# Other starting addresses for the FFN weight tiles and for one SwiGLU remainder

## The chip, the cores and the metric

The kernel runs on one core of a Trainium2 chip. The metric is the device time of one execution in microseconds (us). Before the change it is 1229.76 us, the median of two runs (1229.75 and 1229.76).

## The reference

One layer of a hybrid decoder over 256 tokens of width 2048, in float32:

```python
h = rms_norm(x, attn_norm_w)
p = h @ w_in                                   # 2048 x 6920
mixed = concat(rwkv7(p), gated_deltanet(p), differential_attention(p))
x = x + mixed @ w_out                          # 2048 x 2048
h = rms_norm(x, ffn_norm_w)
gate, up = split(h @ w_ffn_in, 2)              # 2048 x 11264
x = x + (silu(gate) * up) @ w_ffn_out          # 5632 x 2048
```

The change touches the last two products alone, the FFN: 11264 columns going in, 5632 rows coming out.

## The kernel before, in words

**Products in three terms.** Every large product is made of rounded operands (type float32r) and their remainders: a value v becomes hi = round(v) and lo = v - hi, and x*w is taken as xh*wh + xh*wl + xl*wh. In each such matmul the activations are the stationary operand (128 x 128, loaded into the array ahead of the matmul) and the weights are the moving operand (128 x 512, streamed through it). The result goes to a bank of PSUM.

**Weight units.** All weights come as a list of 410 units in the order of their use. A unit is 2 x 128 rows by 512 columns (512 KB; some at the start are smaller). `fetch_upto` issues a unit's DMA from SyncE's queue into a tile `raw`; `stage_upto` lets ScalarE round it into `hi` (L245) and VectorE subtract to `lo` (L246); `products` (L320 to L330) multiplies. A unit of the FFN makes 12 matmuls, all at L328: two halves of the tokens (t), two blocks of 128 rows (k), three terms in the order xh with hi, xh with lo, xl with hi. `take` stages three units ahead of the one that is multiplied (LA = 3), and `hi` and `lo` have four buffers each. In the FFN (units from `plan["far"]` on, which is all but its first four) `raw` comes from the pool `ffn` with FAR + 1 = 9 buffers, fetched five units ahead of staging; elsewhere `raw` has four buffers.

**Order of the work.** Start (`rk` and the LoRA columns, 264 wide), then the other columns of `w_in`; beside them RWKV, the delta net and attention run as generators that advance one step behind each unit; then the output projection (oA, oB) with its stationary operands `mixh_a`/`mixl_a` and `mixh_d`/`mixl_d`; then the FFN in two passes (24 and 20 blocks of 128 hidden columns). A pass makes chunks of 512 gate columns and 512 up columns with `hTh`/`hTl` stationary; SwiGLU's result is transposed by `hid_cols` into `hidh` and, as the remainder, `hidl`; then four output chunks of 512 columns run with `hidh`/`hidl` stationary. Nothing in the FFN is ordered by hand beyond this sequence.

**Where tiles lie.** The pools `raw`, `hi`, `lo` (four tiles of 1024 elements, 4096 bytes in each partition) and `hT` (two tiles of 16 x 256 elements) lie one behind the other, and the pool `ffn` opens directly behind `hT` with `hidh`, `hidl` (24 x 256 elements each). All these sizes are multiples of 512 bytes, and so are the steps between blocks of 128 rows inside them. So in the FFN, and in all products with `hTh`/`hTl` ahead of it whose units are 512 wide, the moving and the stationary operand start a whole multiple of 512 bytes apart. Three cases differ. `mixh_a` and `mixl_a` lie behind tiles that end on an odd 128 bytes (`gns` is 2 x 16 elements): they start 128 bytes past such a multiple. `mixh_d` and `mixl_d` start 160 bytes past one. In the 264-wide units of the start the second block of rows starts 1056 bytes into the tile, 32 bytes past a multiple.

```python
hi = p_hi.tile([P, 1024], F32R, tag="hi", name=nm("hi"))     # stage_upto
lo = p_lo.tile([P, 1024], F32R, tag="lo", name=nm("lo"))
r, h, l = raws.pop(u), hi[:, :nk * n], lo[:, :nk * n]
S.copy(h, r)                                                 # L245
V.tensor_tensor(l, r, h.bitcast(F32), op=ALU.subtract)       # L246
```

Of the kernel before, what the change touches and what calls it, by code (L numbers as in the profile page):

```python
# [9 lines left out]
F32R = mybir.dt.float32r  # L10
# [5 lines left out]
P = 128  # L16
T = 256
# [17 lines left out]
AY = 2  # L35
WARM = 5
FIRST = 8
FAR = 8
START = ((0, 1), (1, 1)) + tuple((k, 2) for k in range(2, 16, 2))

SET_NLE = "natural_log_exp_and_others"
# [52 lines left out]


class Acts:
    """Activation calls grouped by the table set that they need."""

    def __init__(self, tc):
        self.tc, self.nc = tc, tc.nc  # L100
# [27 lines left out]
def trunk(tc, A, out, dbg=None):  # L128
# [24 lines left out]
    def nm(s):  # L153
        uid[0] += 1
        return f"{s}_{uid[0]}"
# [13 lines left out]
        tog[0] ^= 1  # L169
        return rwbank() if tog[0] else gdbank()  # L170

    # ------------------------------------------------------------------ constants
    cst = pc.tile([P, CONST.shape[1]], F32, name="cst")
    vec = pc.tile([P, NV], F32, name="vec")

# [22 lines left out]
    rs1, lnr1, rsq64, ss2, rs2 = rst[:, 0:2], rst[:, 2:4], rst[:, 4:6], rst[:, 6:8], rst[:, 8:10]  # L198
    ssq = pc.tile([P, 8], F32, name="ssq")

    # ------------------------------------------------------------------ weight stream
    cm_raw, p_raw = pool("raw", 4)
    cm_hi, p_hi = pool("hi", 4)
    cm_lo, p_lo = pool("lo", 4)
    LA = 3

    units = []
# [6 lines left out]
    raws, staged = {}, {}  # L214
    state = {"fetched": 0, "next": 0}
# [19 lines left out]
    def stage_upto(i):  # L235
        fetch_upto(min(i + FIRST - LA, 2 * len(START) - 1))
        fetch_upto(i + FAR - LA if i >= plan["far"] else i)
        while state["next"] <= min(i, len(units) - 1):
            u = state["next"]
            srcs, nk, ns = units[u]  # L240
            n = sum(ns)
            hi = p_hi.tile([P, 1024], F32R, tag="hi", name=nm("hi"))
            lo = p_lo.tile([P, 1024], F32R, tag="lo", name=nm("lo"))
            r, h, l = raws.pop(u), hi[:, :nk * n], lo[:, :nk * n]
            S.copy(h, r)  # L245
            V.tensor_tensor(l, r, h.bitcast(F32), op=ALU.subtract)  # L246
            staged[u] = (h.rearrange("p (k c) -> p k c", c=n), l.rearrange("p (k c) -> p k c", c=n))
            state["next"] += 1
# [10 lines left out]
    HALF = (24, 20)  # L259
    plan = {"rk": [], "lora": []}  # L260
# [20 lines left out]
        plan["ffn"].append((h0, nh, ins_, outs_))  # L281
        h0 += nh

    # ------------------------------------------------------------------ side work, emitted between weight units
    jobs = []

    def spawn(gen, steps=0):
# [21 lines left out]
            advance(g)  # L309

    def after(first, then):
        """Keep the order of two instructions of one engine."""
        first, then = getattr(first, "ins", first), getattr(then, "ins", then)
        act._dep(then, first)

    def products(banks, ul, i, xs, n=512, parts=False):
        """What unit i of a chunk adds to its banks."""
        u, k0, nk = ul[i]
        wh, wl = take(u)
        if parts:  # L320
            seq = [(t, k, p_) for k in range(nk) for p_ in range(3) for t in range(2)]
        else:
            seq = [(t, k, p_) for t in range(2) for k in range(nk) for p_ in (0, 2, 1)]
        seen = [0, 0]
        for t, k, p_ in seq:
            seen[t] += 1
            xh, xl = xs(k0 + k)
            state["mm"] = TE.matmul(banks[t][:, 0:n], lhsT=(xl if p_ == 1 else xh)[:, t * P:(t + 1) * P],  # L328
                                    rhs=(wl if p_ == 2 else wh)[:, k, :], start=(i == 0 and seen[t] == 1),
                                    stop=(i == len(ul) - 1 and seen[t] == 3 * nk))  # L330

    def proj(ul, xs):
        """One chunk of 512 columns in token layout: two banks."""
        banks = [mmbank(), mmbank()]
        for i in range(len(ul)):
            products(banks, ul, i, xs)
            tick()
        return banks

    def rsq(out_, in_, scale=1.0, bias=None, b2=None):  # L340
        """out = (in*scale + bias)^-1/2 [* exp(b2)]"""
        act(out_, in_, AF.Ln, scale=scale, bias=eps_c[:in_.shape[0]] if bias is None else bias)
        if b2 is None:
            act(out_, out_, AF.Exp, scale=-0.5)
        else:
            act(out_, out_, AF.Exp, scale=-0.5, bias=b2)

    # ------------------------------------------------------------------ start: x and its norm
    cm_hT, p_hT = pool("hT")
    hTh = p_hT.tile([P, KT, T], F32R, name="hTh")  # L350
    hTl = p_hT.tile([P, KT, T], F32R, name="hTl")
# [6 lines left out]
    cm_x, p_x = pool("xp", side="right")  # L358
    x_in = A["x"].rearrange("(t p) d -> t p d", p=P)
    xT_in = A["xT"].rearrange("(k p) t -> p k t", p=P)  # L360
    # the array's clock rises while the first loads are on their way
    V.memset(xs1, 0.0)
    b = rwbank()
    for _ in range(WARM):
# [1 line left out]
    nc.scalar.dma_start(vec, A["vecs"])  # L366
    act.window(SET_NLE)
    def load_x():
        """x, transposed, in step with the units of the first chunks; then the constants."""
        xTs = {}  # L370

        def fetch_x(q):
            if q < len(START):
                k0, n = START[q]
                xTs[q] = p_x.tile([P, 2, T], F32, tag="xT", name=nm("xT"), bufs=FIRST // 2 + 1)
                (nc.sync if q else nc.scalar).dma_start(xTs[q][:, 0:n, :], xT_in[:, k0:k0 + n, :])
                fetch_upto(2 * q + 1)

        for q in range(FIRST // 2):
            fetch_x(q)  # L380
        for q, (k0, n) in enumerate(START):
            fetch_x(q + FIRST // 2)
            xT = xTs.pop(q)
            xsq = p_x.tile([P, 2, T], F32, tag="xsq", name=nm("xsq"), bufs=2)
            for j in range(n):
                k = k0 + j
                S.activation(hTh[:, k, :], xT[:, j, :], AF.Copy, scale=vcol("attn_w", k))
                V.scalar_tensor_tensor(hTl[:, k, :], xT[:, j, :], vcol("attn_w", k), hTh[:, k, :].bitcast(F32),
                                       op0=ALU.mult, op1=ALU.subtract)
            act(xsq[:, 0:n, :], xT[:, 0:n, :], AF.Square)  # L390
            for j in range(n):
                V.tensor_tensor(xs1, xs1, xsq[:, j, :], op=ALU.add)
            if q < 2:
                stage_upto(2 * q + 1)
            if q:
                yield
        nc.sync.dma_start(cst, A["const"])
        yield
        nc.sync.dma_start(lora[0:64, :], A["w_lora_b"])
        nc.sync.dma_start(lora[64:128, :], A["a_lora_b"])  # L400
        nc.sync.dma_start(glora, A["g_lora_b"])

    def first_norm():
# [7 lines left out]
        V.tensor_scalar(rsq64, rsq64, 1.0 / 64.0, None, op0=ALU.mult)  # L411
        V.tensor_scalar(lnr1, lnr1, -0.5, None, op0=ALU.mult)
        yield
        # small derived vectors
        V.tensor_scalar(omu, vcol("mu", 0, 14), -1.0, 1.0, op0=ALU.mult, op1=ALU.add)
        V.tensor_scalar(oka, vcol("k_a", 0, 4), -1.0, 1.0, op0=ALU.mult, op1=ALU.add)
        V.tensor_scalar(qw8, vcol("qn"), 0.125, None, op0=ALU.mult)
# [22 lines left out]
        products(banks_lora, plan["lora"], i, hx, 264, parts=True)  # L440
    close(cm_x)

    # ------------------------------------------------------------------ RWKV
    cm_tok, p_tok = pool("tok")
    cm_rq, prq = pool("rwq")
    sgx = prq.tile([P, T], F32, name="sgx")
# [27 lines left out]
    kk = pe.tile([P, 4, T], F32, name="kk")  # L474
# [10 lines left out]
    G.memset(XT[96:128, :, 0:32], 0.0)  # L485

    def tokens(banks, n=512):
        """Normalised rows of a chunk, one tile per 128 tokens."""
        res = []
        for t in range(2):  # L490
            tk = p_tok.tile([P, 512], F32, tag="tok", name=nm("tok"), bufs=TOKB)
            S.activation(tk[:, 0:n], banks[t][:, 0:n], AF.Copy, scale=rs1[:, t:t + 1])
            res.append(tk)
        return res

    def turned(toks, i, bank):
        """Column tiles 2i, 2i+1 of a chunk, columns on the partitions: bank[:, j*256 + t]."""
        for j in range(2):
            for t in range(2):
                TE.transpose(bank[:, j * T + t * P:j * T + (t + 1) * P],  # L500
                             toks[t][:, (2 * i + j) * P:(2 * i + j + 1) * P], ident)
        return bank
# [9 lines left out]

    KKRv = KKR.rearrange("p a c s t -> p (a c) s t")

    # inverse of the unit triangular blocks of 32, all at once, by forward substitution
    def forward_sub(n, fill, drain, Fa, Fx, Ft, per):
        scr = tc.dram_tile([n, 32, 32], F32, name=nm("scr"))
        scr2 = tc.dram_tile([n, 32, 32], F32, name=nm("scr2"))
# [142 lines left out]
    def rw_recur():  # L661
        V.transpose(X11[64:96, :, :], XT[64:96, :, 0:32])
        yield
        for i in range(2):
            b = rwbank()
            for j in range(16):
                ch = 16 * i + j
                TE.matmul(b[96:128, j * 32:(j + 1) * 32], lhsT=AHf[64:96, ch, 96:128], rhs=X11[64:96, ch, :],  # L668
                          start=True, stop=True, tile_position=(64, 96))
# [12 lines left out]
            return 2 * hp + par  # L682

        def read(c, which, rows):
            """Chunk c's tokens on the rows given: state times (r or kk), plus the part within the chunk."""
            b = rwbank()
            for hp in range(4):
                if c > 0:
# [62 lines left out]
    ready["rr"] = tokens(proj(plan["rr"], hx))  # L751
    ready["rv"] = tokens(proj(plan["rv"], hx))

    # ------------------------------------------------------------------ gated delta net
    banks_z = proj(plan["gz"], hx)
    while "rw_v" not in ready:
        tick()
# [281 lines left out]
            S.activation(mh, bv, AF.Copy, scale=vcol("gn"))  # L1039
            V.scalar_tensor_tensor(ml, bv, vcol("gn"), mh.bitcast(F32), op0=ALU.mult, op1=ALU.subtract)  # L1040

    # ------------------------------------------------------------------ differential attention
    def diff_evac(j, banks, res):
        qns = []
        for t in range(2):
# [138 lines left out]
            dj = spawn(diff_evac(j, banks, res), 1)  # L1184
        ready["d", g] = ops

    # ------------------------------------------------------------------ output projection
    def mixs(k):
        if k < 8:
            return mixh_a[:, k, :], mixl_a[:, k, :]  # L1190
# [46 lines left out]
    for cm in (cm_d, cm_mixrg, cm_rq, cm_tok):  # L1237
        close(cm)

    # ------------------------------------------------------------------ feed forward  # L1240
    cm_f, pf = pool("ffn")
    act.window(SET_SILU)
    out_v = out.rearrange("(t p) d -> t p d", p=P)
# [10 lines left out]

    for fi, (hh0, nh, ins_, outs_) in enumerate(plan["ffn"]):
        hh_ = pf.tile([P, HALF[0], T], F32R, tag="hidh", name=nm("hidh"))
        hl_ = pf.tile([P, HALF[0], T], F32R, tag="hidl", name=nm("hidl"))
        for c, (ug, uu) in enumerate(ins_):
            bg = proj(ug, hx)
            sgs = []  # L1260
# [67 lines left out]
```

## Time and profile before

| | |
|---|---|
| median of the runs | 1229.76 us |
| the profiled execution: span from the first to the last instruction | 1227.3 us |
| TensorE matmul (PE) busy | 1221.7 us, 6062 instructions |
| TensorE weight load (PEld) busy | 1006.7 us |
| VectorE (DVE) busy | 710.2 us |
| ScalarE (ACT) busy | 589.8 us |
| mean granted TensorE clock | 0.999 |

The profiled execution's span is 1227.3 us; the 2.46 us up to the median lie before its first and behind its last instruction. A matmul's busy time in this profile (some 390 ns) is longer than the time after which the next one starts, because matmuls are pipelined; what a row of matmuls costs is read from the distance of their starts, called the pitch below.

### The profile page before, as it was taken

Reading aid. Unit: us, or ns where it says so; the run is one execution under the profiler, and the core shown is the slowest. Engines: PE = TensorE matmul, PEld = TensorE weight load, DVE = VectorE, ACT = ScalarE, POOL = GpSimd, SP = SyncE. Lnnn points to the kernel's source line nnn. Section 1 sums busy time; section 2 is a strip of 40 time slices with the busy share of each in tenths; the row PEclk is TensorE's granted clock in tenths of the full one; section 3 lists DMA queues with packets and bytes.
Section 4 is the critical chain, followed back from the end, with each engine's and each line's share of the span. In section 5 each row is a group of like instructions: output and inputs, shape, how many; then the busy total and the mean of one; then the engine's idle time right before and its main releaser. Section 6 shows DMA issues by size and latency. Waiting matters only on the chain.

```text
span 1227.3 us, 15743 instructions
## 1 busy us (share of the span) xinstructions
PE 1221.7 (100%) x6062; PEld 1006.7 (82%) x6062; DVE 710.2 (58%) x972; ACT 589.8 (48%) x799; POOL 5.8 (0%) x11
## 2 busy tenths in 40 slices
PE   9999999999999999999999999999999999999998
PEld 8887888788888878888888888888888888888887
DVE  8585965699565766554454454544445445545553
ACT  7764454665446556544444444433344444444332
POOL 0100000000000000000000000000000000000000
PEclk9999999999999999999999999999999999999999
DMA  9755564256555545766666666566666666665660
GB/s 323 211 150 157 167 196 118 72 152 187 174 162 188 164 129 172 280 199 189 186 190 190 189 188 191 188 194 196 193 190 189 191 188 188 195 190 185 212 195 34
DMA packets 125082, 222.41 MB, mean 181 GB/s; under 512 B 15664, under 2 KB 19888, under 8 KB 125008
## 3 DMA queue, kind: packets, MB, share of 16 engines
q1 hardware_dynamic: 116848, 217.15, 58.6%
q10 hardware_dynamic: 8160, 4.27, 1.2%
q8 instruction: 47, 0.77, 0.2%
q14 instruction: 27, 0.22, 0.1%
HBM read 218.50 MB, written 2.88 MB: 180 GB/s over the span
## 4 chain that ended last, share of the span: by engine, by line
PE 99%; DMA 1%; ACT 0%; DVE 0%; issue 0%; SPq 0%
PE mm L328 90%; PE rw L500 1%; PE gd L500 1%; PE rw L692 1%; PE rw L622 1%; PE rw L1085 1%; PE rw L689 0%; PE rw L705 0%; DMA xT<-in_xT 0%; PE rw L562 0%; DMA vec<-in_vecs 0%; PE rw L1120 0%; PE gd L1120 0%; PE rw L676 0%; PE rw L668 0%; ACT s L121 0%
## 5 line engine op out<-in xcount | busy, mean ns | idle before, releaser
L246 DVE TENSOR_TENSOR lo<-raw,hi 128x1024 fp32r<-128x1024 f32 (+2 forms) x410 | 493.9, 1208 | 432.8 <-ACT hi L245 429.0
L245 ACT CAST hi<-raw 128x1024 fp32r<-128x1024 f32 (+2 forms) x410 | 425.2, 1039 | 535.3 <-PE mm L328 509.7
L328 PE MATMUL mm<-hi,hTh 128*128 128x512 f32 (+1 forms) x1152 | 448.9, 394 | 0.2
L328 PE MATMUL mm<-hi,hTl 128*128 128x512 f32 (+1 forms) x1152 | 441.4, 388 | 0.0
L328 PE MATMUL mm<-lo,hTh 128*128 128x512 f32 (+1 forms) x1152 | 441.1, 387 | 0.0
L328 PEld LDWEIGHTS mm<-hi,hTh 128*128 128x128 f32 x1152 | 215.6, 188 | 44.6 <-issue 1.1
L328 PEld LDWEIGHTS mm<-hi,hTl 128*128 128x128 f32 x1152 | 215.2, 188 | 45.1 <-issue 0.6
L328 PEld LDWEIGHTS mm<-lo,hTh 128*128 128x128 f32 x1152 | 215.4, 188 | 42.8 <-issue 1.1
L328 PE MATMUL mm<-hi,hidh 128*128 128x512 f32 x352 | 137.3, 390 | 0.0
L328 PE MATMUL mm<-hi,hidl 128*128 128x512 f32 x352 | 137.0, 389 | 0.0
L328 PE MATMUL mm<-lo,hidh 128*128 128x512 f32 x352 | 137.0, 389 | 0.0
L328 PEld LDWEIGHTS mm<-hi,hidl 128*128 128x128 f32 x352 | 66.1, 188 | 13.9
L328 PEld LDWEIGHTS mm<-hi,hidh 128*128 128x128 f32 x352 | 66.1, 188 | 13.6
L328 PEld LDWEIGHTS mm<-lo,hidh 128*128 128x128 f32 x352 | 66.1, 188 | 13.5
L328 PE MATMUL mm<-hi,mixh_a 128*128 128x512 f32 x64 | 26.0, 406 | 0.0
L328 PE MATMUL mm<-hi,mixh_d 128*128 128x512 f32 x64 | 25.9, 408 | 0.0
L328 PE MATMUL mm<-hi,mixl_d 128*128 128x512 f32 x64 | 25.4, 400 | 0.0
L328 PE MATMUL mm<-lo,mixh_d 128*128 128x512 f32 x64 | 25.4, 396 | 0.0
L328 PE MATMUL mm<-hi,mixl_a 128*128 128x512 f32 x64 | 25.3, 395 | 0.0
L328 PE MATMUL mm<-lo,mixh_a 128*128 128x512 f32 x64 | 25.2, 394 | 0.0
L121 ACT ACTIVATE sg<-mm,rst 128x512 f32<-128x512 f32 x22 | 15.2, 691 | 10.7 <-PE mm L328 10.7
L778 DVE SCALAR_TENSOR_TENSOR cacc<-gd,vec,cacc 128x255 f32<-128x255 f32 (+2 forms) x36 | 16.2, 477 | 5.8 <-ACT cacc L776 5.5
(301 smaller groups left out, 729.4 us busy)
## 6 DMA issues: line engine op xcount, KB each, us to landing
raw<-in_w_ffn_in SPq DMA_DIRECT2D x176, 512.0 KB, 3.8
raw<-in_w_in SPq DMA_DIRECT2D x103, 512.0 KB, 3.7
raw<-in_w_ffn_out SPq DMA_DIRECT2D x88, 512.0 KB, 4.5
raw<-in_w_out SPq DMA_DIRECT2D x32, 512.0 KB, 4.0
raw<-in_w_in SPq DMA_DIRECT2D x9, 256.0 KB, 5.7
xr<-in_x SPq DMA_DIRECT2D x8, 256.0 KB, 5.1
out<-xr ACTq DMA_DIRECT2D x8, 256.0 KB, 3.7
xT<-in_xT SPq DMA_DIRECT2D x7, 256.0 KB, 5.6
```

What stands on the lines that cost most here:

```text
L121: r = self.nc.scalar.activation(out, in_, func, **kw)
L245: S.copy(h, r)
L246: V.tensor_tensor(l, r, h.bitcast(F32), op=ALU.subtract)
L328: state["mm"] = TE.matmul(banks[t][:, 0:n], lhsT=(xl if p_ == 1 else xh)[:, t * P:(t + 1) * P], rhs=(wl if p_ == 2 else wh)[:, k, :], star ...
L500: TE.transpose(bank[:, j * T + t * P:j * T + (t + 1) * P], toks[t][:, (2 * i + j) * P:(2 * i + j + 1) * P], ident)
L622: TE.matmul(b[:, hp * P:(hp + 1) * P], lhsT=KB[rows, hp, c, :, :].rearrange("p s t -> p (s t)"), rhs=KKR[rows, hp, c, :, :].rearrange("p s ...
L692: TE.matmul(b[rows, h * 64:(h + 1) * 64], lhsT=AH[:, c, h % 2, h // 2, 64 * which:64 * which + 64], rhs=VU[:, c, h, :], start=(c == 0 and ...
L778: V.scalar_tensor_tensor(acc[:, sft:T], src[:, 0:T - sft], vcol("conv", 4 * ct + 3 - sft), acc[:, sft:T], op0=ALU.mult, op1=ALU.add)
L1085: TE.matmul(bk[m][:, hx_ * W:(hx_ + 1) * W], lhsT=qT[r, h, i * P:(i + 1) * P], rhs=kT_[r, h, 0:W], start=True, stop=True)
```

## The change

In the FFN's units from `plan["far"]` on, `hi` and `lo` come from the pool `ffn` with three buffers each instead of the four of the older pools, and are 64 elements longer (4352 bytes). What a unit writes begins o = 4 * (u // 2 % 16) elements into them, that is 0, 16, 32, ... 240 bytes, one position for two units and all sixteen in 32 units. `raw` of these units has four buffers (FAR = 3) and is fetched when it is staged. `hidl` is 8 elements longer and its content starts 32 bytes into it. All that is allocated in that pool behind `hidl` lies 32 bytes further on as well. The rest of the diff removes comments.

```diff
-FAR = 8
+FAR = 3
...
-            hi = p_hi.tile([P, 1024], F32R, tag="hi", name=nm("hi"))
-            lo = p_lo.tile([P, 1024], F32R, tag="lo", name=nm("lo"))
-            r, h, l = raws.pop(u), hi[:, :nk * n], lo[:, :nk * n]
+            if u >= plan["far"]:
+                hi = pf.tile([P, 1024 + 64], F32R, tag="hif", name=nm("hi"), bufs=3)
+                lo = pf.tile([P, 1024 + 64], F32R, tag="lof", name=nm("lo"), bufs=3)
+                o = 4 * (u // 2 % 16)
+            else:
+                hi = p_hi.tile([P, 1024], F32R, tag="hi", name=nm("hi"))
+                lo = p_lo.tile([P, 1024], F32R, tag="lo", name=nm("lo"))
+                o = 0
+            r, h, l = raws.pop(u), hi[:, o:o + nk * n], lo[:, o:o + nk * n]
...
-        hl_ = pf.tile([P, HALF[0], T], F32R, tag="hidl", name=nm("hidl"))
+        hl_ = pf.tile([P, HALF[0] * T + 8], F32R, tag="hidl", name=nm("hidl"))
+        hl_ = hl_[:, 8:].rearrange("p (k t) -> p k t", t=T)
```

## Rows read from the trace of the kernel before

**Rows 1.** The page's first part: busy time and instructions of each engine.

```profile
PE 1221.7 (100%) x6062; PEld 1006.7 (82%) x6062; DVE 710.2 (58%) x972; ACT 589.8 (48%) x799; POOL 5.8 (0%) x11
```

**Rows 2.** The chain of work that ended last, by engine (page, part 4).

```profile
PE 99%; DMA 1%; ACT 0%; DVE 0%; issue 0%; SPq 0%
```

**Rows 3.** The page's DMA issues: count, size, us from issue to landing.

```profile
raw<-in_w_ffn_in SPq DMA_DIRECT2D x176, 512.0 KB, 3.8
...
raw<-in_w_ffn_out SPq DMA_DIRECT2D x88, 512.0 KB, 4.5
```

**Rows 4.** Stretches of matmuls alone; (x) counts all that reach into a stretch.

```profile
core 0: us, PE busy (x) PEld busy (x) DVE busy (x) ACT busy (x) POOL busy (x), PEclk, DMA share, GB/s
70.50:75.50 5.00, 5.00 (x24) 4.14 (x23) 4.88 (x6) 4.98 (x7) 0.78 (x1) 1.00 0.11 42
801.00:850.00 49.00, 49.00 (x218) 40.58 (x217) 23.42 (x21) 18.99 (x18) 0.00 (x0) 1.00 0.62 192
419.80:426.50 6.70, 6.70 (x30) 5.41 (x29) 4.76 (x9) 4.95 (x18) 0.00 (x0) 1.00 0.23 81
479.80:486.80 7.00, 7.00 (x32) 5.63 (x31) 5.42 (x7) 3.98 (x8) 0.00 (x0) 1.00 0.64 191
```

**Rows 5.** Order of time, first and last matmul of 801 to 850 (start, duration).

```profile
800.65 0.39 PE L328 MATMUL mm<-hi,hidl 128*128 128x512 f32 x1
...
849.84 0.39 PE L328 MATMUL mm<-hi,hidh 128*128 128x512 f32 x1
```

**Rows 6.** Order of time, first and last matmul of 70.5 to 75.5.

```profile
70.25 0.39 PE L328 MATMUL mm<-hi,hTl 128*128 128x512 f32 x1
...
75.46 0.39 PE L328 MATMUL mm<-lo,hTh 128*128 128x512 f32 x1
```

**Rows 7.** Order of time, output projection oA, 419.8 to 426.5.

```profile
419.58 0.39 PE L328 MATMUL mm<-hi,mixl_a 128*128 128x512 f32 x1
419.81 0.40 PE L328 MATMUL mm<-hi,mixh_a 128*128 128x512 f32 x1
420.05 0.39 PE L328 MATMUL mm<-lo,mixh_a 128*128 128x512 f32 x1
...
426.34 0.40 PE L328 MATMUL mm<-lo,mixh_a 128*128 128x512 f32 x1
```

**Rows 8.** Order of time, output projection oB, 479.8 to 486.8.

```profile
479.45 0.39 PE L328 MATMUL mm<-hi,mixh_d 128*128 128x512 f32 x1
...
479.91 0.40 PE L328 MATMUL mm<-hi,mixl_d 128*128 128x512 f32 x1
480.15 0.39 PE L328 MATMUL mm<-hi,mixh_d 128*128 128x512 f32 x1
...
486.68 0.39 PE L328 MATMUL mm<-lo,mixh_d 128*128 128x512 f32 x1
```

**Rows 9.** Order of time at the start, 264 wide; two matmuls of equal operands merged.

```profile
30.62 0.40 PE L328 MATMUL mm<-hi,hTh 128*128 128x264 f32 x2
...
31.34 0.41 PE L328 MATMUL mm<-hi,hTh 128*128 128x264 f32 x2
...
32.07 0.39 PE L328 MATMUL mm<-hi,hTh 128*128 128x512 f32 x1
```

**Rows 10.** Order of time in the FFN behind two transposes.

```profile
543.76 0.38 PE L500 MATMUL rw<-cst,sg 128*128 128x128 f32 x2
543.90 0.48 PE L328 MATMUL mm<-hi,hTh 128*128 128x512 f32 x1
544.21 0.39 PE L328 MATMUL mm<-lo,hTh 128*128 128x512 f32 x1
...
545.83 0.39 PE L328 MATMUL mm<-hi,hTl 128*128 128x512 f32 x1
```

**Rows 11.** The page's costliest groups, staging: busy us, mean ns, idle before, releaser.

```profile
L246 DVE TENSOR_TENSOR lo<-raw,hi 128x1024 fp32r<-128x1024 f32 (+2 forms) x410 | 493.9, 1208 | 432.8 <-ACT hi L245 429.0
L245 ACT CAST hi<-raw 128x1024 fp32r<-128x1024 f32 (+2 forms) x410 | 425.2, 1039 | 535.3 <-PE mm L328 509.7
```

## The prediction

> **What bounds the kernel now.** I read the busy times first: TensorE is busy for 1221.7 of 1227.3 us, no other engine above 58% of the span [rows 1]. Then the chain of waits: 99% of it is TensorE, nothing else reaches 2% [rows 2]. So the time is the number of matmuls times their pitch, and only what changes one of the two counts. The number stays: the FFN is 176 + 88 units [rows 3] of 12 matmuls, 3168 in all.
>
> The pitch I read from the order of time, in stretches without transposes. In the FFN, 218 matmuls reach into 801 to 850 us, the first starts at 800.65, the last at 849.84: 217 steps, 49.19 / 217 = 0.2267 us, at a granted clock of 1.00, the 2.4 GHz level [rows 4, 5]. At 70 us, with the same multiples of 512 bytes between moving and stationary operand, it is 23 steps in 5.21 us, 0.2265, although ScalarE and VectorE are busy there for 4.98 and 4.88 of 5.00 us [rows 4, 6]. The output projection is slower in the same instruction: oA, its stationary operand 128 bytes off such a multiple, takes 29 steps in 6.76 us, 0.2331, with single steps of 0.23 and 0.24 in turn [rows 4, 7]; oB, 160 bytes off, 31 steps in 7.23 us, 0.2332, where two of 0.23 and one of 0.24 repeat [rows 4, 8]. Clock, columns and line are the same; the other engines, busier at 70 us, don't explain it. What differs in the code is where the operands lie against each other. That is an inference from three places, but it is exactly the quantity that this change moves, in 16-byte steps.
>
> **The change, part by part.**
>
> *Longer way through fewer buffers.* Rounding waits for the array to give back a buffer of hi (L245, 509.7 us of idle ended by PE) [rows 11], so with three buffers it starts one unit later, when the unit three before is done. Two units then lie between that and its use: 2 x 12 x 0.2267 = 5.44 us. Rounding and subtracting take 1.04 + 1.21 = 2.25 us [rows 11], so 3.2 us are left, and the work that hides them is two units of matmuls. SiLU, the SwiGLU products and the copies of the transposes stand on the same two engines at each chunk's end; they may take those 3.2 us. If the cover were gone, TensorE would wait at most once a unit for what sticks out. I cost it at 0. Bounds: nothing and, at 22 ends of a gate or up chunk, one rounding of 1.04 us each, 23 us; I take nothing, since both engines sit idle for over 400 us ahead of exactly these instructions [rows 11].
>
> *Four raw buffers.* A raw tile comes free when its remainder is formed, and the next DMA into it is issued then, on SyncE's queue, where only other weight loads stand. It lands 3.8 to 4.5 us later [rows 3]. By the order above it is issued 2.25 us after the end of unit v - 7 and needed for rounding at the end of unit v - 3, that is 4 x 2.72 = 10.9 us: 4.1 us of cover remain. Cost 0. The copies' and subtractions' start addresses change too; neither engine bounds anything.
>
> *The addresses.* The first four FFN units keep the old tiles, so 260 x 12 = 3120 matmuls get moving operands at o = 0 to 240 bytes; buffers of 4352 bytes (17 x 256) and a pool moved by 32 bytes add multiples of 32. So against hTh/hTl, and against hidh, all 16-byte positions within 256 bytes occur, equally often as far as the list of units goes round; hidl stands 32 bytes from where hidh stands. The pitch at most positions isn't in the trace. The nearest rows: 226.7 ns at 0, 233.1 at 128, 233.2 at 160. For 32 bytes there are only matmuls of 264 columns: six from 30.62 to 31.34 at distance 0 and six up to 32.07 at 32 bytes, 0.72 and 0.73 us [rows 9], so about 1 ns more each. None of these is below the value at 0.
>
> I take the mean of the three 512-column values, 231.0 ns, for the sixteen positions: zero is one of them and may have good neighbours, as the 264-wide rows say, and the two far ones agree. That is 4.3 ns x 3120 = 13 us. A second effect points the same way: after a disturbance the pitch needs several matmuls to settle. Behind two transposes the first takes 0.31 us, and the seven steps from 544.21 to 545.83 average 0.231 before 0.227 returns [rows 10]. Each new position (every two units) disturbs it anew; that holds up a good position as much as the mean already does, so I add nothing.
>
> Bounds of a matmul: above, the slow step of oB, 0.24 us by the rounded starts [rows 8], held throughout would be some 11 ns x 3120 = 34 us. Below, 512 columns without any fixed part: from 264 to 512 columns the pitch rises from 0.12 (0.72 / 6) to 0.2267, 0.43 ns a column, or 220 ns for 512, 6.9 ns less each, -21 us.
>
> Sum against the profiled execution: 1227.3 + 13 = 1240.3 us of span; 2.46 us lie around it up to the median of the runs, which makes 1243.
>
> **Rivals.**
>
> *Addresses don't matter.* The slower pitch of the output projection would then come from something else there. For it: attention runs beside oA. Against: oB keeps the pattern, and 70 us is as busy. The time would be that of before, 1228 to 1232; chance 0.16. The Trainium skill speaks for this one: by "SBUF — State Buffer", section "Who interferes with whom", TensorE has two SBUF read ports, one for the moving operand and one for the weight load, independent of each other, and never waits on another engine. By that rule the position could cost nothing and the sum would be 0. The two pitches of rows 5 and 7 are the measurement that it leaves unexplained.
>
> *Distance zero is the bad case and most positions are free.* Both operands then meet in the same part of the memory at 0, and 128 and 160 bytes happen to meet it again; an offset of 16 to 112 bytes keeps them apart. For it: 226.7 ns is above the 220 of the columns alone, so something is being paid at 0. Against: all three other distances seen are slower. It decides if more than about half of the positions lie below 226.7 ns. At 220 to 225 the FFN gains 1.7 to 6.7 ns a matmul, 5 to 21 us: 1209 to 1225; chance 0.16. The same skill, "TensorE: Matmul & The Clock Gate", section "Back-to-back issue gap", gives an estimate further down, about 216 ns for 512 columns, -34 us; no row here goes that low.
>
> *Never settled, and late staging.* Every move of the position throws the pitch up to between oB's mean and its slow step, 235 to 238 ns, and two units are too short to come back: 8 to 11 ns x 3120, 25 to 34 us. Or the chunk ends stick out by 1 us each: 13 + 23 = 36 us. Either way 1254 to 1266; chance 0.12. For it: seven matmuls to settle out of 24. Against: they average 231 [rows 10], not 235.
>
> **How the numbers follow.** The forecast, a pitch between 229 and 234 averaged over the FFN (1236 to 1253), has 0.56; likeliest 1243. The range 1222 to 1255 takes in the forecast, the case without effect, the mild part of the gain and the start of the late one; outside lie about 0.10 below and 0.10 above. A measurement of this kernel tells about 2% (24.6 us) from no change: 0.05 for faster than 1205, since even 220 ns throughout gives 1209; 0.13 for slower than 1254; the rest within.
>
> **What would show it.** After: stretches of FFN matmuls whose pitch changes every second unit (24 matmuls) with the position, and returns after 32 units; a mean near 231 with clock 1.00; 227 where the distance is 0 and 233 near 128 and 160; the stages before the FFN unchanged to 1 us; no idle time of TensorE behind rounding or DMA. I am wrong if the pitch stays at 226.7 at every position, if some positions lie well below it, or if TensorE waits for hi, lo or raw.

## The result and the profile after

The changed kernel takes 1245.51 us (1245.22 to 1245.81, two runs) against 1229.76: 1.0128 times as long, 95% interval 1.0085 to 1.0172. Forecast was 1243 in a range of 1222 to 1255. The profiled execution has a span of 1243.4 us, 16.1 more than before; the sum had 1240.3.

Busy times, the chain of waits by engine and the two staging groups of the changed kernel:

```profile
PE 1236.4 (99%) x6062; PEld 1006.8 (81%) x6062; DVE 710.0 (57%) x972; ACT 588.5 (47%) x799; POOL 5.8 (0%) x11
...
PE 99%; DMA 1%; ACT 0%; DVE 0%; SPq 0%; issue 0%; ACTq 0%
...
L252 DVE TENSOR_TENSOR lo<-raw,hi 128x1024 fp32r<-128x1024 f32 (+2 forms) x410 | 493.8, 1208 | 452.6 <-ACT hi L251 452.0
L251 ACT CAST hi<-raw 128x1024 fp32r<-128x1024 f32 (+2 forms) x410 | 423.8, 1036 | 562.3 <-PE mm L334 537.6
```

Same number of matmuls, 14.7 us more of TensorE, nothing else busier [rows 1, 2, 11]: rounding and subtracting at the shifted starts take 1036 and 1208 ns as before. All time in which TensorE waited, with its releaser (total, times, longest):

```profile
PE rw L371 <- DVE xs L368: 1.2, 1, 1.2
PE mm L334 <- ACT hi L251: 1.1, 1, 1.1
PE mm L334 <- ACT hTh L393: 0.7, 1, 0.7
```

Each occurs once, in the first 40 us; in the FFN TensorE waits for nothing. Now the FFN's first and last matmul in order of time, first of the kernel before, then of the changed one:

```profile
493.61 0.40 PE L328 MATMUL mm<-hi,hTh 128*128 128x512 f32 x1
...
1222.99 0.39 PE L328 MATMUL mm<-hi,hidl 128*128 128x512 f32 x1
```

```profile
493.99 0.40 PE L334 MATMUL mm<-hi,hTh 128*128 128x512 f32 x1
...
505.85 0.40 PE L334 MATMUL mm<-hi,hTh 128*128 128x512 f32 x1
...
511.49 0.39 PE L334 MATMUL mm<-hi,hTh 128*128 128x512 f32 x1
...
517.08 0.40 PE L334 MATMUL mm<-hi,hTh 128*128 128x512 f32 x1
...
522.53 0.40 PE L334 MATMUL mm<-hi,hTh 128*128 128x512 f32 x1
...
528.01 0.39 PE L334 MATMUL mm<-hi,hTh 128*128 128x512 f32 x1
...
533.57 0.40 PE L334 MATMUL mm<-hi,hTh 128*128 128x512 f32 x1
...
607.89 0.40 PE L334 MATMUL mm<-hi,hTh 128*128 128x512 f32 x1
...
613.34 0.40 PE L334 MATMUL mm<-hi,hTh 128*128 128x512 f32 x1
...
1239.13 0.40 PE L334 MATMUL mm<-hi,hidl 128*128 128x512 f32 x1
```

What ran before the FFN differs by 0.38 us. The FFN takes 745.14 us against 729.38: 15.76 us more, all of the change. The FFN's weight tiles step through their positions from 505.85 on. The rows from there to 533.57 are the first matmuls of successive pairs of units, 24 matmuls apart. In the allocated layout the moving operand lies 208 bytes past the stationary one (modulo 256) from 505.85 on, then 224, 240, 0 and 16. The five stretches last 5.64, 5.59, 5.45, 5.48 and 5.56 us: a pitch of 235.0, 232.9, 227.1, 228.3 and 231.7 ns. The pitch steps with the position, and in these input products the old 226.7 [rows 5] is kept, but for the first matmuls that settle, at 240 and 0 alone (176 and 192 always have transposes among their matmuls here, 48 and 64 but once). One round of the list later the distances are the same but for a multiple of 256 bytes, and so is the stretch at 240: 5.45 us from 607.89.

The output products keep it nowhere. Here is their pair with `hidh` at distance 0, where `hidl` lies 32 bytes off:

```profile
795.06 0.40 PE L334 MATMUL mm<-hi,hidh 128*128 128x512 f32 x1
...
800.66 0.39 PE L334 MATMUL mm<-hi,hidh 128*128 128x512 f32 x1
```

It takes 5.60 us, 233.3 ns a matmul.

A stretch of output products, columns as in rows 4:

```profile
820.00:850.00 30.00, 30.00 (x131) 24.34 (x130) 14.35 (x13) 11.54 (x11) 0.00 (x0) 1.00 0.59 186
```

The granted clock is 1.00 as before, and the 30 us hold some 129 matmuls where 226.7 ns would give 132.

### The profile page after: what moved, and what is told of

Its sections match the earlier page's. It is cut to its first block, busy times and chain, and to the rows that moved or that the text cites. A ratio compares the mean times of both kernels' runs of the same rounds, so it can differ in the third digit from the quotient of the medians.

```text
span 1243.4 us, 15743 instructions
## 1 busy us (share of the span) xinstructions
PE 1236.4 (99%) x6062; PEld 1006.8 (81%) x6062; DVE 710.0 (57%) x972; ACT 588.5 (47%) x799; POOL 5.8 (0%) x11
## 4 chain that ended last, share of the span: by engine, by line
PE 99%; DMA 1%; ACT 0%; DVE 0%; SPq 0%; issue 0%; ACTq 0%
PE mm L334 90%; PE rw L506 1%; PE gd L506 1%; PE rw L698 1%; PE rw L628 1%; PE rw L1091 1%; PE rw L695 0%; DMA raw<-in_w_in 0%; PE rw L711 0%; PE rw L568 0%; DMA vec<-in_vecs 0%; PE rw L1126 0%; PE gd L1126 0%; PE rw L682 0%; PE rw L674 0%; ACT s L121 0%
## 5 line engine op out<-in xcount | busy, mean ns | idle before, releaser
L252 DVE TENSOR_TENSOR lo<-raw,hi 128x1024 fp32r<-128x1024 f32 (+2 forms) x410 | 493.8, 1208 | 452.6 <-ACT hi L251 452.0
L251 ACT CAST hi<-raw 128x1024 fp32r<-128x1024 f32 (+2 forms) x410 | 423.8, 1036 | 562.3 <-PE mm L334 537.6
```

## Experiments

All edits are against the changed kernel or the kernel before, as said. Times are compared with the kernel before on the same chip.

**Buffers alone.** The changed kernel without its two shifts (the tiles keep their 64 spare elements):

```diff
-                o = 4 * (u // 2 % 16)
+                o = 0
...
-        hl_ = pf.tile([P, HALF[0] * T + 8], F32R, tag="hidl", name=nm("hidl"))
-        hl_ = hl_[:, 8:].rearrange("p (k t) -> p k t", t=T)
+        hl_ = pf.tile([P, HALF[0], T], F32R, tag="hidl", name=nm("hidl"))
```

> The changed kernel without any shift: three hi and lo buffers and four raw buffers from the pool of the FFN, but every unit begins at the start of a 1024-element tile and the SwiGLU remainder isn't moved, so moving and stationary operand of the FFN lie multiples of 256 bytes apart again. Theory (the distance between the two operands sets the pitch): FFN pitch 226.7 ns at every unit, time 1230 us (1228 to 1232). Rival (the shorter way through fewer buffers costs the time): pitch 226.7 ns with waits of TensorE for hi or raw, 1240 to 1246 us.

Measured 1229.88 us, ratio 0.9997 (0.9988 to 1.0006). Its first and last matmul of the FFN:

```profile
494.81 0.40 PE L334 MATMUL mm<-hi,hTh 128*128 128x512 f32 x1
...
1224.19 0.39 PE L334 MATMUL mm<-hi,hidl 128*128 128x512 f32 x1
```

729.38 us, the same as before to 0.01 us. Three buffers and the short fetch cost nothing; the rival falls. What is left is the place of the operands.

**The remainder alone.** The kernel before, with hidl's 32 bytes as in the change and nothing else.

> The kernel before with the remainder hidl moved by 32 bytes alone. Theory: only the 1056 matmuls of the FFN's output products change. Where the changed kernel had hidh at distance 0 and hidl 32 bytes beside it, its three terms took 231.4, 232.0 and 235.2 ns, 232.9 on the mean, so 6.2 ns x 1056 = 6.5 us: 1236 us (1234 to 1238). Rival (only the moving tiles' own start counts): 1230 us.

Measured 1236.87 us, 1.0048 (1.0036 to 1.0061). The three terms in order of time:

```profile
800.85 0.40 PE L328 MATMUL mm<-hi,hidh 128*128 128x512 f32 x1
801.08 0.40 PE L328 MATMUL mm<-lo,hidh 128*128 128x512 f32 x1
801.32 0.39 PE L328 MATMUL mm<-hi,hidl 128*128 128x512 f32 x1
...
803.65 0.40 PE L328 MATMUL mm<-hi,hidh 128*128 128x512 f32 x1
```

Twelve matmuls from 800.85 to 803.65 take 2.80 us, 233.3 ns each. The moving tiles are untouched; where the stationary operand lies counts too, at the price that was forecast.

**One far position.** The first experiment with `o = 52` (208 bytes) for every unit.

> The layout of the first experiment, but every unit from the fifth of the FFN on begins 208 bytes into its tile: one fixed distance in place of sixteen. Theory: the distance holds a pitch of its own; at 208 bytes the changed kernel's three terms took 234.9, 234.9 and 234.5 ns, so 8.1 ns x 3120 = 25 us, 1255 us (1252 to 1258), the same at the end of a chunk as at its start. Rival (moving from one position to the next disturbs the pitch, a fixed one settles back to 227 ns): 1230 us, at most 1233.

Measured 1252.38 us, 1.0177 (1.0163 to 1.0191), at the lower end of the 1252 to 1258 expected. A stretch of matmuls alone and its first and last:

```profile
810.00:850.00 40.00, 40.00 (x172) 32.11 (x171) 18.47 (x16) 14.92 (x15) 0.00 (x0) 1.00 0.58 184
```

```profile
809.66 0.40 PE L334 MATMUL mm<-lo,hidh 128*128 128x512 f32 x1
...
849.78 0.40 PE L334 MATMUL mm<-lo,hidh 128*128 128x512 f32 x1
```

171 steps in 40.12 us, 234.6 ns, 40 us long without a move: a position holds its own pitch. It isn't the moving from one to the next that costs.

**A map of pairs.** The first experiment with separate starts for hi and lo.

```diff
-                o = 0
+                j = (u - plan["far"]) // 2
+                o, ol = 4 * (j % 16), 4 * ((j // 16 + 0) % 16)
...
-            r, h, l = raws.pop(u), hi[:, o:o + nk * n], lo[:, o:o + nk * n]
+            r, h, l = raws.pop(u), hi[:, o:o + nk * n], lo[:, ol:ol + nk * n]
```

> The layout of the first experiment with separate starts for hi and lo: hi moves by 16 bytes every two units, lo by 16 bytes every 32 units (0 to 112 bytes), so that 128 pairs of distances are seen for two units each. Theory: pitch by the distance of each moving tile from the stationary operand loaded beside it; 226.7 ns where both are 0, some 229 to 236 ns elsewhere, 1243 to 1249 us. It is open whether a pair lies below 226.7 ns: by the theory that 0 is the best distance none does; by the rival that something is still being paid at 0, some reach 220 to 225 ns.

One run: 1245.14 us. The two quickest pairs of units, hi and lo both at 0, and hi at 192 with lo at 16, each with the start of the pair behind it:

```profile
506.49 0.39 PE L335 MATMUL mm<-hi,hTh 128*128 128x512 f32 x1
...
511.93 0.39 PE L335 MATMUL mm<-hi,hTh 128*128 128x512 f32 x1
...
664.64 0.39 PE L335 MATMUL mm<-hi,hTh 128*128 128x512 f32 x1
...
670.09 0.40 PE L335 MATMUL mm<-hi,hTh 128*128 128x512 f32 x1
```

5.44 and 5.45 us for 24. No pair was quicker, so the second rival of the prediction (0 is the bad distance) has no position on its side. Only half of lo's positions were tried, and pairs with transposes among their matmuls can't be compared. The second of the two pairs also tells against the theory: neither of its moving tiles is at distance 0 or 240, and it is as quick as those.

**One operand, the other, both.** The first experiment, with the output products' weight tiles 48 bytes on (`o = 12` for units of w_ffn_out), with hidh and hidl 48 bytes on, and with both. For both:

```diff
-                o = 0
+                o = 12 if units[u][0][0].tensor is w_fo.tensor else 0
...
-        hh_ = pf.tile([P, HALF[0], T], F32R, tag="hidh", name=nm("hidh"))
-        hl_ = pf.tile([P, HALF[0], T], F32R, tag="hidl", name=nm("hidl"))
+        hh_ = pf.tile([P, HALF[0] * T + 64], F32R, tag="hidh", name=nm("hidh"))
+        hh_ = hh_[:, 12:12 + HALF[0] * T].rearrange("p (k t) -> p k t", t=T)
+        hl_ = pf.tile([P, HALF[0] * T + 64], F32R, tag="hidl", name=nm("hidl"))
+        hl_ = hl_[:, 12:12 + HALF[0] * T].rearrange("p (k t) -> p k t", t=T)
```

> The layout of the first experiment with the weight tiles of the FFN's output products alone begun 48 bytes later; hidh and hidl stay. Theory (the distance between moving and stationary operand sets the pitch, with a period of 256 bytes): distance 48; at 48 the input products of the changed kernel took 233.6, 232.3 and 233.2 ns, so 6.4 ns x 1056 = 6.7 us, 1236 to 1237 us. Rival (the start of the moving operand by itself counts): the same here.

> The layout of the first experiment with hidh and hidl begun 48 bytes later; the weight tiles stay at the start of theirs. Theory: distance -48, which is 208 of 256 bytes; the pitch there was 234.8 ns, 8.1 x 1056 = 8.6 us, 1238 to 1239 us. Rival (only the moving operand's own start counts): 1230 us.

> The layout of the first experiment with both operands of the FFN's output products begun 48 bytes later: the distance is 0 again, while neither start is where it was. Theory: pitch 226.7 ns, 1230 us (1229 to 1231). Rival (each operand's own start counts, not the distance): 1236 to 1237 us if it is the moving one's, about 1245 us if both cost what they cost alone.

Measured 1232.92 (1.0027, 1.0017 to 1.0038), 1236.65 (1.0056, 1.0044 to 1.0069) and 1235.09 us (1.0046, 1.0032 to 1.0059). The stretch from 801 to 850, in this order:

```profile
801.00:850.00 49.00, 49.00 (x214) 39.99 (x214) 23.36 (x20) 18.41 (x18) 0.00 (x0) 1.00 0.62 192
```

```profile
801.00:850.00 49.00, 49.00 (x211) 39.87 (x210) 22.23 (x20) 18.90 (x18) 0.00 (x0) 1.00 0.61 184
```

```profile
801.00:850.00 49.00, 49.00 (x211) 39.48 (x210) 22.72 (x20) 18.61 (x18) 0.00 (x0) 1.00 0.62 187
```

214, 211 and 211 matmuls reach in where it was 218 [rows 4]. The second came out near its expectation (6.9 of 8.6 us), the first at half (3.3 of 6.7), and the third, 1235 instead of 1230, refutes the theory in its simple form: the distance is 0 and the pitch isn't 226.7. The rivals fare no better (the moving operand's own start would leave the second at 1230; both costs added make 1240). In the stretch shown of the second run nothing that another engine reads or writes starts elsewhere modulo 256 bytes, so it is TensorE's own operand that costs.

The third run shows one thing more. In its second pass the starts are the same modulo 256 bytes, and the pitch isn't:

```profile
1140.00:1189.00 49.00, 49.00 (x214) 39.83 (x213) 23.76 (x23) 18.88 (x18) 0.00 (x0) 1.00 0.68 210
```

214 matmuls reach in where 211 did in the first pass, 231.1 ns a step against 233.3. In both passes the trace shows the pitch going from one of these values to the other behind a group of four transposes: in the second pass from 231 to 233 ns at 1123 us and back at 1126, from where it holds to the end. So the places alone don't settle it; what ran before takes part.

**Rows of positions.** What the stationary operand's own place does: hidh and hidl moved by one amount in each pass, the output products' weight tiles stepping through all sixteen positions.

```diff
-                o = 0
+                q = plan["outs"].get(u)
+                o = 0 if q is None else 4 * (q % 16)
...
+        ou = [u_ for l_ in outs_ for u_, _, _ in l_]
+        plan.setdefault("outs", {}).update({u_: i_ // 2 for i_, u_ in enumerate(ou)})
...
+        sh = (16, 32)[fi]
+        hh_ = pf.tile([P, HALF[0] * T + 64], F32R, tag="hidh", name=nm("hidh"))
+        hh_ = hh_[:, sh:sh + HALF[0] * T].rearrange("p (k t) -> p k t", t=T)
```

That is 64 and 128 bytes; hidl likewise. The second run has (4, 8), the third (12, 48).

> The distance alone didn't explain the last three runs: with both operands 48 bytes on the output products' pitch was 232.6 ns, not 226.7. Here hidh and hidl begin 64 bytes later in the first pass and 128 bytes later in the second, and the weight tiles of the output products step through all sixteen 16-byte positions, two units each. Theory A (both starts have to be multiples of 64 bytes and the distance a multiple of 256): 226.7 ns where the moving operand has moved as far as the stationary one, 229 to 236 ns elsewhere. Theory B (the place of the stationary operand within 256 bytes decides by itself): no position at 226.7 ns in either pass. Theory C (the distance alone): 226.7 ns where both moved equally, as A, but also in the next two runs.

> The same with hidh and hidl 16 bytes later in the first pass and 32 bytes later in the second. Theory A: above 228 ns everywhere, equal shifts included. Theory C: 226.7 ns at equal shifts of 16 and of 32 bytes. Theory B: no position at 226.7 ns.

> The same with 48 bytes later in the first pass and 192 bytes later in the second. Theory A: at equal shifts 232.6 ns in the first pass, as when the whole stage was moved by 48 bytes, and 226.7 ns in the second. Theory B: above 228 ns in both. Theory C is refuted at 48 already.

One run each: 1235.07, 1235.16 and 1233.71 us. First matmuls of three successive pairs of units each: moved by 64 bytes (first run), by 16 and by 32 (second run), by 48 (third run). In each triple the distance is -16 in the first pair (240 of 256) and 0 in the second; the third row ends it.

```profile
778.61 0.40 PE L337 MATMUL mm<-hi,hidh 128*128 128x512 f32 x1
...
784.06 0.40 PE L337 MATMUL mm<-hi,hidh 128*128 128x512 f32 x1
...
789.54 0.39 PE L337 MATMUL mm<-hi,hidh 128*128 128x512 f32 x1
```

```profile
851.51 0.39 PE L337 MATMUL mm<-hi,hidh 128*128 128x512 f32 x1
...
856.95 0.39 PE L337 MATMUL mm<-hi,hidh 128*128 128x512 f32 x1
...
862.47 0.39 PE L337 MATMUL mm<-hi,hidh 128*128 128x512 f32 x1
...
1212.82 0.40 PE L337 MATMUL mm<-hi,hidh 128*128 128x512 f32 x1
...
1218.27 0.40 PE L337 MATMUL mm<-hi,hidh 128*128 128x512 f32 x1
...
1223.75 0.39 PE L337 MATMUL mm<-hi,hidh 128*128 128x512 f32 x1
```

```profile
861.17 0.39 PE L337 MATMUL mm<-hi,hidh 128*128 128x512 f32 x1
...
866.61 0.39 PE L337 MATMUL mm<-hi,hidh 128*128 128x512 f32 x1
...
872.13 0.39 PE L337 MATMUL mm<-hi,hidh 128*128 128x512 f32 x1
```

Moved by 64 and by 32 bytes, the two stretches last 5.45 and 5.48 us, just as in the changed kernel; at 128 (first run, from 1156.95) and 192 (third run, from 1177.98) they do so too. Moved by 16 and by 48 they last 5.44 and 5.52: the floor (the lowest pitch seen, 226.7) at -16, but 230 ns at 0. At 48 the floor also occurs where the changed kernel is slower, at distance 112 (and at 16 likewise):

```profile
816.93 0.39 PE L337 MATMUL mm<-hi,hidh 128*128 128x512 f32 x1
...
822.37 0.40 PE L337 MATMUL mm<-hi,hidh 128*128 128x512 f32 x1
```

That pair takes 5.44 us. So theory A falls (32 is no multiple of 64 and reaches the floor), B falls (the floor occurs in every pass), and C falls at 16 and 48. What fits all three runs is the distance modulo 256 together with the amount, modulo 32 bytes, by which the stationary operand was moved: 32, 64, 128 and 192 give one list of sixteen pitches, 16 and 48 another, each to within half a ns away from transposes. It doesn't fit everything: in the third run the pair at distance 0 with 48 bytes took 230 ns, where the stage held there throughout (the run with both moved) makes 210 steps in 49.0 us in its first pass, 233 ns, and 231 in its second; and the map has a quick pair outside the list.

**The projection.** The kernel before, with the output projection's stationary operands at distance 0 as well.

```diff
-    mixh_a = p_mixrg.tile([P, 8, T], F32R, name="mixh_a")
+    mixh_a = p_mixrg.tile([P, 8 * T + 32], F32R, name="mixh_a")
+    mixh_a = mixh_a[:, 32:].rearrange("p (k t) -> p k t", t=T)
...
-        mixl_d = pdr.tile([P, 8, T], F32R, name="mixl_d")
+        mixl_d = pdr.tile([P, 8 * T + 40], F32R, name="mixl_d")
+        mixl_d = mixl_d[:, 0:8 * T].rearrange("p (k t) -> p k t", t=T)
```

> The kernel before with the stationary operands of the output projection moved so that they too lie a multiple of 256 bytes from the moving ones (mixh_a and mixl_a by 128 bytes, mixh_d and mixl_d by 160); the FFN as before. Theory: the 384 matmuls of the projection fall from 233.2 to 226.7 ns, 6.5 x 384 = 2.5 us: 1227.3 us. Rival (the projection is slower because attention runs beside it): 1229.8 us.

Measured 1228.19 us, 0.9987 (0.9979 to 0.9996): the quickest version here, by little. From the projection's first matmul to the FFN's first, before and here:

```profile
387.53 0.50 PE L328 MATMUL mm<-hi,mixh_a 128*128 128x512 f32 x1
```

```profile
388.21 0.50 PE L328 MATMUL mm<-hi,mixh_a 128*128 128x512 f32 x1
...
492.70 0.39 PE L328 MATMUL mm<-hi,hTh 128*128 128x512 f32 x1
```

493.61 - 387.53 = 106.08 us became 104.49: 1.6 us of the 2.5. The projection of the kernel before was slower for its place, with attention beside it as ever: 31 matmuls reach into 419.8 to 426.5 us here, 30 before [rows 4]. The gain is smaller in short rows: the 48 matmuls from 392.22 fall from 235.4 to 229.4 ns a step, the twelve from 388.21 from 241.3 to 238.7. That the pitch has to settle behind each disturbance fits this; nothing here tests it by itself.

**Half the load.** What is the pitch of 226.7 ns made of?

```diff
-            state["mm"] = TE.matmul(banks[t][:, 0:n], lhsT=(xl if p_ == 1 else xh)[:, t * P:(t + 1) * P],
+            w = 64 if p_ and units[u][0][0].tensor is w_fo.tensor and i < len(ul) - 1 else P
+            state["mm"] = TE.matmul(banks[t][0:w, 0:n], lhsT=(xl if p_ == 1 else xh)[:, t * P:t * P + w],
```

> The kernel before; in the FFN's output products the two remainder terms (xh with lo, xl with hi) load and multiply only the first 64 of the 128 tokens of a half, in all units but a chunk's last (640 matmuls of 1056 load 64 columns instead of 128). This leaves out those terms for the other tokens. The question is what is paid at the lowest pitch seen, 226.7 ns, against 213.3 ns for 512 columns at 2.4 GHz. Theory (the load of the stationary operand takes time from the moving stream, so half the load takes half of the 13.3 ns): 6.7 ns x 640 = 4.3 us less, 1225.5 us. Rival (a fixed cost of each matmul): 1229.8 us.

Measured 1232.68 us, 1.0026 (1.0017 to 1.0035): slower. Its stretch from 801 to 850, and the mean length of a full and of a short load:

```profile
801.00:850.00 49.00, 49.00 (x215) 32.92 (x214) 23.37 (x20) 18.37 (x18) 0.00 (x0) 1.00 0.62 192
```

```profile
L329 PEld LDWEIGHTS mm<-hi,hidh 128*128 128x128 f32 x352 | 66.0, 188 | 31.9
L329 PEld LDWEIGHTS mm<-hi,hidl 128*64 128x64 f32 x320 | 43.0, 134 | 30.2
```

The short loads are 54 ns shorter in the record, yet 215 matmuls reach in where 218 did. Less loading didn't give time back; the steps, 226 or 227 ns each before, range from 224 to 236 instead and average 229. Both theories miss, and what the floor consists of stays open.

## Why the prediction was right, point by point

- **Bound.** The time is the count of matmuls times their pitch: the count stayed, 15.76 of the 16.1 us lie in the FFN, without a wait.
- **Buffers, four raw tiles: 0.** Right, 729.38 us of FFN with and without them. The cover of one unit less was enough, as worked out from the 5.44 us of two units.
- **The output projection as the sign of it.** Right: moved to distance 0, it became 1.6 us quicker.
- **Addresses: 4.3 ns on 3120 matmuls, 13 us.** Right in sign and cause; mis-sized by a sixth. It measured 15.76 / 3120 = 5.05 ns. At 128 and 160 the sweep has 232 and 234 ns (5.57 us from 567.87, 5.62 from 579.03), near the 233 of the projection. But two of sixteen distances stay at the floor in the input products and none in the output products, not a third of the mean as the three rows weighted it; the others run from 229 to 235. With two of sixteen at the floor and the rest at the rows' 233.1 the same sum would have given 5.6 ns and 17.6 us. So the good places are rarer than taken. Against that, the other places cost less on the mean than the rows' value, and the 22 moved pairs of units with transposes lose only 3.5 ns a matmul (1.8 us in all). The errors partly cancel: that the sum came so near is in part luck. The good neighbour that the 264-wide rows hinted at 32 bytes isn't there: 32 is one of the slow distances with 512 columns, and the good one here lies at -16.
- **The bounds of a matmul** have two slips. A step of 0.24 us is 13.3 ns above 226.7, not 11, and makes 41 us, not 34; and 264 to 512 columns at 0.43 ns a column make 220.3 ns, 6.4 below it and 20 us, not 6.9 and 21. The far ends of two rivals, 1266 and 1209 us, rest on such numbers; the forecast doesn't.
- **The remainder's 32 bytes** had no term of their own. Alone they cost 1.0048; in the change they are part of the 5.05.
- **Never settled:** no. Held throughout, 208 has the pitch that it has for two units in the sweep (234.6 and 235.0 ns); it costs more than the sweep only because 208 is one of the worst.
- **Addresses don't matter:** no. The Trainium skill's "SBUF — State Buffer", section "Who interferes with whom", gives TensorE two independent read ports; the trace shows that this does not make the operands' places free: with nothing else changed, the start alone moved a run by 0.3 to 1.8%.
- **What was too strong:** "the quantity" was named as the distance. The move of both operands by 48 bytes shows that the distance alone doesn't decide, and its two passes that the places alone don't either. Why the places count at all stays open.

## What to carry to other kernels

Where rounded float32 matmuls of 512 columns stream back to back, read the pitch from the starts, stage by stage: a stage whose pitch is some per cent above another's, at the same clock, may only have its tiles elsewhere. Keeping moving and stationary tiles a multiple of 256 bytes apart, with the stationary one a multiple of 32 bytes from its place in the kernel before, gave the lowest pitch seen or one within 2 ns of it; a single odd-sized tile ahead of them can lose it. Change such a thing alone, since buffers and depths that come with it can be free.

## What the runs showed of the hardware

- The pitch of a 128 x 512 float32r matmul depends on where its operands start: 227 ns at best and 235 at worst over the pairs of units without transposes in the sweep of the changed kernel, 226.7 in the kernel before, at granted clock 1.00. It came back the same where the distance differed by a multiple of 256 bytes (5.45 us for 24 matmuls at 240, and one round later again).
- No position's mean went below 226.7 ns: not the sixteen of the change, not the pairs of the map, not the sixteen in each of six places of the stationary operand.
- The same place need not give one pitch: distance 48 took 5.59 us for 24 matmuls in the first run of rows (from 800.70), 233 ns, but held throughout a stage (the moving operand 48 bytes on) 213 steps took 49.0 us, 230 ns. With both operands 48 bytes on, one stage ran at 233.3 ns in its first pass and at 231.1 in its second, at the same starts modulo 256 bytes, and went from one to the other behind transposes. How the pattern depends on what ran before wasn't tested further.
